# A recurrence's level in one matmul burst for each unit and step, and the merge's GELUs ordered behind the level's copies

## The chip, the cores and the metric

The kernel runs on one core of a Trainium2 chip. Time is the device time of one execution in microseconds (us). A run of the kernel before gave 1525.88 us as the median of three (1525.83 to 1526.22). The five engines have a queue each, worked off in order: TensorE (PE, matmuls), VectorE (DVE), ScalarE (ACT), GpSimd (POOL) and SyncE (SP); here POOL and SP mostly start DMAs.

## The reference

One layer of a hybrid decoder, batch 1, 1024 positions, width 1024, all in float32:

```
h    = rms_norm(x);  proj = h @ w_in            # RWKV r,k,v and low-rank parts | S5 input u | two gates
g_rwkv, g_s5 = split(sigmoid(proj[...] + b_gate))
o_rwkv = rwkv7_branch(...) @ w_branch_rwkv      # 8 heads of 64: S = S*w + (S a) b^T + v k^T ; y = S r
y      = gelu(s5_scan(u));  o_s5 = (y * sigmoid(y @ w_glu + b_glu)) @ w_branch_s5
x = x + rms_norm((g_rwkv * o_rwkv + g_s5 * o_s5) @ w_out)
x = x + rms_norm((gelu(gate) * val) @ w_down)   # gated MLP, width-3 convolution over time before the gelu
```

## The kernel before

**Three stages.** The input projection with the S5 scan comes first (to about 370 us), then the RWKV recurrence (about 370 to 770 us), then the MLP. The change lies in the recurrence.

**The recurrence.** The 8 heads are worked off in four passes, i = 0 to 3: one group of four heads for one half of the time axis each. A pass holds two units u of two heads. Time is cut into chunks of 64 positions, 8 in a pass. A pass goes through these parts:

- `rwkv_front` (prep, on PE, DVE, ACT): decay factors, the normalised keys (L736 to L741 make the operands `ar` and `bk`), and the products of all pairs of positions within a chunk (matmuls L752, masked by DVE L754 into `gr`). L760 stores the part that has to be inverted (`md`).
- `rwkv_inv`: the triangular systems of all chunks are solved for blocks of 32 by 62 small DVE operations that hang on each other (L810 and L812, 31 of each). POOL stores the result (`xd`, L815) and loads it back into `gr` (L822).
- `rwkv_nat`: transposes of `bk` and of the values (L782 to L792).
- `rwkv_level` joins the blocks of 32 to inverses of 64. DVE transposes (L835), then come two steps: matmuls of 32x32 (L838) whose results ACT copies to SBUF (L839), then matmuls L840 on these copies, whose results ACT copies into `gr` (L841).
- `rwkv_chain`: eight chunks one after the other, each in three stages: a (L888, L870), b (L899, L901) and c (L906, L911), with small copies by ACT and DVE between. After every second chunk `moments` makes means and squares (L924 to L927; the square is ACT's L926).

In the text "level 2" is `rwkv_level` of pass 2, while the prep of pass 3 runs beside it.

**The fill.** All the small matmuls wait for other engines. In their gaps PE does k-steps: three matmuls of 128x128 on 128x512 (L180 to L182) of the large products. Fill in pass 2: the last gate tiles, then `merge`. `merge` first makes gate tiles; with the second and the third of them it also emits GELUs of the S5 result for batches 0, 1 and 2, 3 (`s5_y`: DMA, then GELU L1254; `s5_split`: ACT's cast L1261 to the high part `hh`, DVE's subtraction L1262 to the low part `hl`). After the third gate tile comes the first GLU tile (`MGAP`), whose four k-steps read the four pairs `hh`, `hl`. The buffers `ev` for the GELUs are three.

**What sets the order.** PE's order is written out by the program's own planner, `drive`. Lanes (chain, two prep lanes) yield how much work they have issued, when they may go on, and a weight; a lane's work takes 0.8 x work x weight from a credit, and each k-step gives 0.68 back. While the credit is below zero only fill is emitted. The order on the other engines is set by a scheduler from priorities (fill loads and weights above chain, chain above prep) and its own model of times; a manual dependency only orders one instruction behind another on the same engine. `s5_y` orders each GELU behind `self.squared`, an instruction that `rwkv_front` sets (its Square, L700). GELU needs a table of ACT's that is loaded ahead of the first one (ACT_TABLE_LOAD).

Of the kernel before, what the change touches and what calls it, by code (L numbers as in the profile page):

```python
# [73 lines left out]
class Kern:  # L74
# [749 lines left out]
    def rwkv_level(self, d, spare):  # L824

        A, V = self.nc.scalar, self.nc.vector
        mm = self.nc.tensor.matmul
        gr = d["gr"]
        p0 = self.chk(1).rearrange("p (u c t) -> p u c t", u=2, t=32)
        p0, p1 = [p0[:, u] for u in range(2)], [self.chb().rearrange("p (c t) -> p c t", t=32) for u in range(2)]  # L830
        xz = (self.tg("x", 1, pool=self.rka) if spare else self.tg("ld", NLD)).rearrange("p (u c t) -> p u c t", u=2, t=32)
        top, bot = [[slice(64 * h + o, 64 * h + o + 32) for h in range(2)] for o in (0, 32)]
        t0, t1 = slice(0, 32), slice(32, 64)
        for h, sl in enumerate(top):
            self.levelled = V.transpose(xz[sl].rearrange("p u c t -> p (u c) t"), gr[sl, :, :, h, t0].rearrange("p u c t -> p (u c) t"))  # L835
        yield 0, T_LT
        kw = dict(stop=True, skip_group_check=True)
        steps = ((lambda u, c, h: mm(p1[u][bot[h], c], gr[top[h], u, c, h, t1], xz[top[h], u, c], start=c == 0, **kw),  # L838
                  lambda u, h: A.copy(xz[bot[h], u], p1[u][bot[h], 0:8])),  # L839
                 (lambda u, c, h: mm(p0[u][top[h], c], xz[bot[h], u, c], gr[bot[h], u, c, h, t1], start=c == 0, **kw),  # L840
                  lambda u, h: A.copy(gr[top[h], u, :, h, t1], p0[u][top[h], 0:8])))  # L841
        for step, evict in steps:
            for u in range(2):
                for c in range(8):
                    for h in range(2):
                        step(u, c, h)
                    if c % 4 == 3:
                        yield 0.3, 0.3, 2.0
                for h in range(2):
                    evict(u, h)  # L850
            yield 0, T_LV

    def rwkv_chain(self, d):
# [1339 lines left out]
```

## Time and profile before

| what | value |
|---|---|
| median of the runs | 1525.88 us (1525.83 to 1526.22) |
| profiled execution, its own time | 1524.13 us |
| its span | 1522.3 us |
| PE busy | 1469.8 us (97%) |
| DVE, ACT, POOL busy | 1158.5 (76%), 726.6 (48%), 180.2 us (12%) |

A row of a timeline gives start and duration in us, engine, line, operation, output <- input with their shapes, the number of instructions taken together (x), and in brackets how long the engine was idle before and which engine, tile and line ended it. A small matmul counts as two or more records, so a burst of 8 reads x16. In the table by stretches the columns are the stretch and its length, busy time and instructions of PE, its weight loads (PEld), DVE, ACT and POOL, the clock granted to PE (1.00 is full), the share of the DMA engines, and GB/s.

### The profile page before, as it was taken

What the parts mean: (1) busy time and instruction counts of PE and PEld (TensorE: products, weight loads), DVE (VectorE), ACT (ScalarE), POOL (GpSimd) and SP (SyncE); (2) the same over time, 40 slices, a digit from 0 to 9 for tenths busy, and PEclk for the clock granted to TensorE, in tenths of its full rate; (3) what the DMA queues carried; (4) which work ended last, traced back from release to release, by engine and by line L of the source; (5) the groups of instructions that cost most, each with busy time, mean ns of one, the idle gap of its engine ahead of it and who ended that gap; (6) DMA issues with size and microseconds to landing.
All of it is one profiled execution on the core that took longest, in us unless ns stands there. A gap on an engine that the chain in (4) does not pass through costs nothing.

```text
span 1522.3 us, 23902 instructions
## 1 busy us (share of the span) xinstructions
PE 1469.8 (97%) x8804; PEld 1166.1 (77%) x8804; DVE 1158.5 (76%) x2157; ACT 726.6 (48%) x1209; POOL 180.2 (12%) x340
## 2 busy tenths in 40 slices
PE   7999999999999998999999999999999999999997
PEld 5788787787677675666788778888888887888875
DVE  7989974765655594975767888888888888698767
ACT  5465444331453434556635555555555555444451
POOL 0022111124021232030110010000000000000000
PEclk9999999999999998999999999999999999999999
DMA  6455344444332446452456575233333336944712
GB/s 211 135 154 159 98 139 145 143 135 152 107 124 96 128 120 192 146 167 70 157 189 199 182 242 180 93 108 117 113 110 117 112 109 225 333 154 138 246 59 111
DMA packets 121558, 225.26 MB, mean 148 GB/s; under 512 B 31024, under 2 KB 37168, under 8 KB 121440
## 3 DMA queue, kind: packets, MB, share of 16 engines
q1 hardware_dynamic: 90576, 154.77, 32.5%
q0 software_dynamic: 21024, 64.71, 12.9%
q10 hardware_dynamic: 9840, 4.24, 1.1%
q8 instruction: 69, 1.13, 0.3%
q14 instruction: 49, 0.40, 0.1%
HBM read 164.16 MB, written 57.41 MB: 146 GB/s over the span
## 4 chain that ended last, share of the span: by engine, by line
PE 44%; DVE 4%; DMA 4%; ACT 1%; issue 1%; SPq 0%; DVEq 0%; ACTq 0%
PE d L1779 8%; PE rp L1600 5%; PE rp L1602 5%; PE rp L1601 5%; PE mm L1602 2%; PE mm L1600 2%; PE mm L1601 2%; DMA st<-in_w_down_dram 2%; PE ch L181 1%; PE mm L180 1%; PE ch L182 1%; PE mm L181 1%; PE gm L180 1%; PE ch L180 1%; PE mm L182 1%
## 5 line engine op out<-in xcount | busy, mean ns | idle before, releaser
L180 PE MATMUL gm<-hh,wh 128*128 128x512 f32 x672 | 283.1, 421 | 1.9 <-DVE ev L1057 1.9
L181 PE MATMUL gm<-hl,wh 128*128 128x512 f32 x672 | 264.9, 394 | 0.1
L182 PE MATMUL gm<-hh,wl 128*128 128x512 f32 x672 | 264.7, 394 | 0.0
L160 ACT CAST wh<-wf 128x512 fp32r<-128x512 f32 x181 | 111.9, 619 | 171.5 <-PE gm L181 88.5
L161 DVE TENSOR_TENSOR wl<-wf,wh 128x512 fp32r<-128x512 f32 x181 | 124.3, 690 | 86.5 <-ACT wh L160 84.5
L180 PEld LDWEIGHTS gm<-hh,wh 128*128 128x128 f32 x672 | 127.0, 189 | 34.3 <-issue 4.0
L182 PEld LDWEIGHTS gm<-hh,wl 128*128 128x128 f32 x672 | 127.0, 189 | 28.1
L181 PEld LDWEIGHTS gm<-hl,wh 128*128 128x128 f32 x672 | 127.4, 190 | 22.5 <-DVE hl L246 1.0
L1779 PE MATMUL d<-xh,wl 128*128 128x512 f32 x308 | 113.5, 392 | 2.1 <-DVE wl L246 2.1
L1779 PE MATMUL d<-xh,wh 128*128 128x512 f32 x308 | 113.9, 393 | 1.1 <-DVE zg L1630 1.1
L1779 PE MATMUL d<-xl,wh 128*128 128x512 f32 x308 | 113.4, 392 | 0.6 <-DVE xl L246 0.6
L1600 PE MATMUL rp<-t,h 128*128 128x512 f32 x252 | 98.3, 390 | 1.4 <-ACT p L1614 1.4
L1602 PE MATMUL rp<-t,l 128*128 128x512 f32 x252 | 98.0, 389 | 0.0
L1601 PE MATMUL rp<-t,h 128*128 128x512 f32 x252 | 98.0, 389 | 0.0
L1779 PEld LDWEIGHTS d<-xh,wl 128*128 128x128 f32 x308 | 58.1, 189 | 15.1 <-DVE wl L246 2.9
L1779 PEld LDWEIGHTS d<-xh,wh 128*128 128x128 f32 x308 | 57.8, 189 | 14.2 <-DVE zg L1630 1.5
L246 DVE TENSOR_TENSOR l<-r,h 128x1024 fp32r<-128x1024 f32 (+1 forms) x40 | 38.9, 971 | 38.9 <-ACT h L245 38.9
L1779 PEld LDWEIGHTS d<-xl,wh 128*128 128x128 f32 x308 | 58.2, 189 | 13.2 <-DVE xl L246 0.9
L245 ACT CAST h<-r 128x1024 fp32r<-128x1024 f32 (+1 forms) x40 | 33.9, 849 | 69.5 <-PE rp L1601 67.2
L1621 DVE SCALAR_TENSOR_TENSOR y<-zv,vecs,y 128x1023 f32<-128x1023 f32 (+1 forms) x42 | 53.7, 1280 | 10.2 <-ACT y L1619 10.2
L1600 PEld LDWEIGHTS rp<-t,h 128*128 128x128 f32 x252 | 47.3, 188 | 11.9 <-ACT p L1614 2.2
L1601 PEld LDWEIGHTS rp<-t,h 128*128 128x128 f32 x252 | 47.3, 188 | 9.8
(476 smaller groups left out, 3338.1 us busy)
## 6 DMA issues: line engine op xcount, KB each, us to landing
r<-in_w_up_dram SPq DMA_DIRECT2D x42, 512.0 KB, 3.5
wf<-in_w_in_dram SPq DMA_DIRECT2D x72, 256.0 KB, 3.1
st<-in_w_down_dram SPq DMA_DIRECT2D x55, 256.0 KB, 4.3
st<-ACT SPq DMA_DIRECT2D x44, 256.0 KB, 4.2
ACT<-y POOLq DMA_DIRECT2D x21, 512.0 KB, 2.9
GT<-ev POOLq DMA_DIRECT2D x32, 256.0 KB, 3.5
wf<-in_w_br_dram SPq DMA_DIRECT2D x32, 256.0 KB, 3.4
wf<-in_w_out_dram SPq DMA_DIRECT2D x32, 256.0 KB, 2.8
```

What stands on the lines that cost most here:

```text
L160: self.last_wh = nc.scalar.copy(h[:, :n], f[:, :n])
L161: low = nc.vector.tensor_tensor(l[:, :n], f[:, :n], h[:, :n].bitcast(F32), ALU.subtract)
L180: mm(ps, a, xh[k], start=a0, stop=False)
L181: mm(ps, a, xl[k], start=False, stop=False)
L182: mm(ps, b, xh[k], start=False, stop=z0)
L245: a = self.nc.scalar.copy(hi, x)
L246: self.split_ops = a, (eng or self.nc.vector).tensor_tensor(lo, x, hi.bitcast(F32), ALU.subtract)
L1600: mm(ps, wh[:, c], xh, start=first and k == 0, stop=False, skip_group_check=True)
L1601: mm(ps, wh[:, c], xl, start=False, stop=False, skip_group_check=True)
L1602: mm(ps, wl[:, c], xh, start=False, stop=k == 3, skip_group_check=True)
L1621: V.scalar_tensor_tensor(y[:, lag:], z[:, 0:1024 - lag], self.vec(nme, i), y[:, lag:], ALU.mult, ALU.add)
L1779: mm(ps, w[:, c], y[:, x], start=start and k == 0, stop=stop and k == 2, skip_group_check=True)
```

## The change

Two places in `rwkv_level`:

```
                 for c in range(8):
                     for h in range(2):
                         step(u, c, h)
-                    if c % 4 == 3:
-                        yield 0.3, 0.3, 2.0
+                yield 0.6, 0.3, 1.5
                 for h in range(2):
-                    evict(u, h)
+                    self.squared = evict(u, h)
             yield 0, T_LV
```

The 16 matmuls of a unit and step are issued together, and one yield stands for two. A unit and step then takes 0.8 x 0.6 x 1.5 = 0.72 from the credit where it took 2 x 0.8 x 0.3 x 2.0 = 0.96. `self.squared` now is also set by the level's copies, and so GELUs that are emitted later stand behind the last copy emitted. The file is one line shorter: L850 and later lines have a number lower by one after the change (GELU L1253, cast L1260, split L1261, square L925).

What moves in level 2 is seen at three places. First ACT, from the end of the gate tiles on; `chb` is what L838 wrote, `ev` the GELUs' buffers, `hh` the high parts. Before:

```order
L1139 ACTIVATE ev_6167<-gm_6096,hb_b_gate 128x512
L1254 ACT_TABLE_LOAD
L1254 ACTIVATE ev_6274<-ev_6274 128x512
L1254 ACTIVATE ev_6281<-ev_6281 128x512
L1261 CAST hh_6277<-ev_6274 128x512
L160 CAST wh_6566<-wf_6568 128x512
L1261 CAST hh_6284<-ev_6281 128x512
L1254 ACTIVATE ev_6336<-ev_6336 128x512
L839 COPY x_6155<-chb_6154 32x256
L1261 CAST hh_6339<-ev_6336 128x512
```

The level's copies stood behind the table load and three GELUs. After the change the same GELUs come in chunk 1 of the chain, behind its square:

```order
L925 ACTIVATE ar_4784<-yn_6426 128x256
L1253 ACT_TABLE_LOAD
L1253 ACTIVATE ev_6469<-ev_6469 128x512
L160 CAST wh_6804<-wf_6806 128x512
L1260 CAST hh_6472<-ev_6469 128x512
L1253 ACTIVATE ev_6476<-ev_6476 128x512
L1253 ACTIVATE ev_6533<-ev_6533 128x512
L1260 CAST hh_6479<-ev_6476 128x512
L1260 CAST hh_6536<-ev_6533 128x512
L902 COPY UV_5672<-chb_6611 64x128
L873 COPY p_1213_6621<-chk_6610 128x128
L1253 ACTIVATE ev_6540<-ev_6540 128x512
```

Second PE, where the first GLU tile (`gm_6652`) reads them, in chunk 2 after the change; `chk_6610` and `chb_6611` are that chunk's stages b and c:

```order
L900 MATMUL chk_6610<-S_2614,ar_4784 64x64 x4
L180 MATMUL gm_6652<-hh_6472,wh_6646 128x512
L181 MATMUL gm_6652<-hl_6473,wh_6646 128x512
L182 MATMUL gm_6652<-hh_6472,wl_6647 128x512
L180 MATMUL gm_6652<-hh_6479,wh_6646 128x512
L181 MATMUL gm_6652<-hl_6480,wh_6646 128x512
L182 MATMUL gm_6652<-hh_6479,wl_6647 128x512
L905 MATMUL chk_6610<-UV_5672,gr_4604 64x64 x4
L910 MATMUL chb_6611<-UV_5672,bkn_5671 64x64 x4
L180 MATMUL gm_6652<-hh_6536,wh_6646 128x512
```

Between stage c of chunk 1 (L905) and this tile PE has four k-steps and the stages a and b of chunk 2. Before, the first GLU tile stood in chunk 0, and its GELUs ahead of the chain.

Third DVE, at the end of level 2's inverse (tiles `x_5413` before, `x_5426` after). Before:

```order
L737 SCALAR_TENSOR_TENSOR gr_5718<-ld_5722,vecs,rp_6006 128x512
L810 TENSOR_TENSOR tm_5509<-x_5413,mt_5412 128x16
L246 TENSOR_TENSOR hl_6061<-ld_5696,hh_6060 128x512
L812 TENSOR_TENSOR x_5413<-x_5413,tm_5509 128x16
L246 TENSOR_TENSOR hl_6051<-hl_6051,hh_6050 128x512
L246 TENSOR_TENSOR hl_6065<-ld_5699,hh_6064 128x512
L737 SCALAR_TENSOR_TENSOR gr_5718<-ld_5731,vecs,rp_6019 128x512
```

L738, L739 and four of L741 followed. After the change these stand between the inverse's operations, from L737 on; a piece of it:

```order
L810 TENSOR_TENSOR tm_5504<-x_5426,mt_5425 128x98
L741 SCALAR_TENSOR_TENSOR bk_5829<-gr_5687,ld_5693 64x8x64
L812 TENSOR_TENSOR x_5426<-x_5426,tm_5504 128x2x7x7
L741 SCALAR_TENSOR_TENSOR bk_5829<-gr_5687,ld_5702 64x8x64
L810 TENSOR_TENSOR tm_5507<-x_5426,mt_5425 128x84
L741 SCALAR_TENSOR_TENSOR bk_5829<-gr_5687,ld_5702 64x8x64
L812 TENSOR_TENSOR x_5426<-x_5426,tm_5507 128x2x7x6
L246 TENSOR_TENSOR hl_6081<-ld_5665,hh_6080 128x512
L810 TENSOR_TENSOR tm_5510<-x_5426,mt_5425 128x70
L246 TENSOR_TENSOR hl_6085<-ld_5668,hh_6084 128x512
```

Of the 14 operations L737 to L741 and L246, all now stand ahead of the inverse's last row; before, two did. On POOL the three stores of `md` that follow them now stand ahead of the loads L822, where they stood behind, and the GELUs' loads come later.

## The prediction

> **What bounds the kernel now.** First the page: the span and the busy shares.
>
> ```profile
> span 1522.3 us, 23902 instructions
> PE 1469.8 (97%) x8804; PEld 1166.1 (77%) x8804; DVE 1158.5 (76%) x2157; ACT 726.6 (48%) x1209; POOL 180.2 (12%) x340
> ```
>
> TensorE (PE) is the bound: 52.5 us of 1522.3 are idle, and the matmuls themselves stay the same in number and size. So the change can move the time in three ways: the cost of switching between small and large matmuls, PE's waits, and the clock that PE is granted. Next the table by stretches around level 2, the third of the four passes through the edited loop (from about 576 us), and one stretch in level 1; the ninth column is the granted clock.
>
> ```profile
> 460.00:464.00 4.00, 4.00 (x12) 2.88 (x10) 3.90 (x18) 0.69 (x1) 0.55 (x1) 0.58 0.19 70
> 588.00:592.00 4.00, 2.31 (x18) 1.13 (x18) 3.80 (x6) 3.43 (x7) 2.83 (x5) 0.71 0.43 122
> 592.00:596.00 4.00, 4.00 (x38) 2.52 (x38) 1.65 (x2) 1.44 (x3) 2.38 (x6) 0.50 0.60 166
> 596.00:600.00 4.00, 4.00 (x25) 2.78 (x24) 0.00 (x0) 1.44 (x4) 0.94 (x2) 0.51 1.00 230
> ```
>
> From 588 to 600 PE runs at about half speed: 4 x (0.29 + 0.50 + 0.49) = 5.1 us are lost. In 460 to 464 it is 4 x 0.42 = 1.7 us. What came before the slow stretch stands in PE's timeline:
>
> ```profile
> 589.28 0.24 PE L840 MATMUL chk<-gr,x 32*32 32x32 f32 x2 [3.42 <-ACT x L839]
> 589.94 0.63 PE L840 MATMUL chk<-gr,x 32*32 32x32 f32 x14 [0.41 <-ACT x L839]
> ```
>
> PE waits 3.42 + 0.41 = 3.8 us for the copies of L839, the largest wait of the recurrence. ScalarE's (ACT's) timeline says what is ahead of them, and VectorE's (DVE's) when the last result of that block is ready:
>
> ```profile
> 581.66 1.28 ACT L1254 ACT_TABLE_LOAD   x1 [6.03 <-issue]
> 582.96 1.38 ACT L1254 ACTIVATE ev<-ev 128x512 f32<-128x512 f32 x2
> 584.24 1.09 ACT L1261 CAST hh<-ev 128x512 fp32r<-128x512 f32 x1
> 585.23 0.62 ACT L160 CAST wh<-wf 128x512 fp32r<-128x512 f32 x1
> 588.86 1.02 ACT L839 COPY x<-chb 32x256 f32<-32x256 f32 x3
> 591.65 1.06 ACT L1261 CAST hh<-ev 128x512 fp32r<-128x512 f32 x1
> 593.22 1.04 DVE L1262 TENSOR_TENSOR hl<-ev,hh 128x512 fp32r<-128x512 f32 x1
> ```
>
> The merge's table load, GELUs and casts run where the level needs its copies. From table load to last split the block takes 594.26 - 581.66 = 12.6 us.
>
> **The change part by part. The bursts.** Level 0 shows the price of cutting a burst in two:
>
> ```profile
> 376.35 0.44 PE L838 MATMUL chb<-ld,gr 32*32 32x32 f32 x16
> 376.72 0.50 PE L180 MATMUL gm<-hh,wh 128*128 128x512 f32 x1
> 377.06 0.40 PE L181 MATMUL gm<-hl,wh 128*128 128x512 f32 x1
> 377.29 0.39 PE L182 MATMUL gm<-hh,wl 128*128 128x512 f32 x1
> 377.61 0.44 PE L838 MATMUL chb<-ld,gr 32*32 32x32 f32 x16
> ```
>
> Large matmuls start 0.23 us apart (377.06 to 377.29). The one behind a burst holds 0.34 (0.11 more), the one ahead of the next 0.32 (0.09 more): 0.20 us for each visit, while the small matmuls cost the same either way. 32 bursts become 16; in the order, 15 stretches of small matmuls fewer are left. **-3.0 us** (-1.6 if only the 0.11 behind a burst goes, -3.4 if all 16 and a little more).
>
> **The GELUs leave the level.** With them go the waits of 3.8 us and the slow clock: **-3.8** and **-5.1**. The copies now stand behind one tanh that is done well before, and PE has over 4 us of other work between the last L838 and the first L840 (a set of L752, four k-steps and L763), so I leave nothing of this wait. Level 3's wait should go too, since its inverse (DVE) gets all of the new stalls below as extra time: **-1.0** (0 to -1.0).
>
> ```profile
> L838 PE MATMUL chb<-ld,gr 32*32 32x32 f32 x64 | 2.0, 194 | 1.0 <-DVE ld L835 1.0
> ```
>
> **The inverse of level 2 gets company.** This is the side of the change that its words don't tell: in the new order the preparation of pass 3 (L737 to L741) and four splits (L246) stand inside level 2's inverse on DVE, where nearly all of it followed before.
>
> ```profile
> 556.38 1.04 PE L736 MATMUL rp<-csts,gr 128*128 128x128 f32 x8
> 557.86 0.74 DVE L737 SCALAR_TENSOR_TENSOR gr<-ld,vecs,rp 128x512 f32<-128x512 f32 x1
> 559.21 0.19 DVE L812 TENSOR_TENSOR x<-x,tm 128x16 f32<-128x16 f32 x1
> 560.22 0.68 DVE L246 TENSOR_TENSOR hl<-ld,hh 128x512 fp32r<-128x512 f32 x1
> 562.09 1.28 DVE L738 SCALAR_TENSOR_TENSOR ar<-gr 128x512 f32<-128x512 f32 x2
> 563.29 1.28 DVE L739 SCALAR_TENSOR_TENSOR gr<-ld,gr 128x512 f32<-128x512 f32 x2
> 565.70 1.98 DVE L741 SCALAR_TENSOR_TENSOR bk<-gr,ld 64x512 f32<-64x512 f32 x3
> 571.66 0.69 DVE L835 STREAM_TRANSPOSE x<-gr 32x512 f32<-32x512 f32 x1
> 559.69 1.29 POOL L815 DMA_DIRECT2D xd<-x  x2 [0.25 <-DVE x L812]
> 565.79 4.64 POOL L822 DMA_DIRECT2D gr<-xd  x8 [1.09 <-DMA xd<-x]
> 566.88 1.44 PE L752 MATMUL rp<-ar,bk 64*64 64x128 f32 x32
> 576.10 0.44 PE L838 MATMUL chb<-x,gr 32*32 32x32 f32 x16
> ```
>
> The inverse used to end at 559.4. The first L737 can't run before L736 (PE has no earlier place for it), so about 557.6, and now 19 operations of the inverse stand behind it: some 4.6 us (an estimate of 0.24 each, where the last and smallest takes 0.19), and the 14 others (two of which stood there before), both L737 among them, come to 2 x 0.74 + 1.28 + 1.28 + 4 x 0.66 + 4 x 0.68 = 9.4 by these rows, about 8.8 as neighbouring rows overlap a little. It ends near 571.0, 11.6 us later. From its end to the loads of L822 took 6.4 us and those 4.6 more; both transposes of L835 add 1.4, so L838 can start at about 583.4. Three DMAs of `md` now stand ahead of L822 on POOL's queue, and they end in the 2 us in which it waits for `xd` anyway. PE comes to L838 at 576.1 + 1.7 (a set of L752 and a k-step, 1.0 and 0.7, now stand ahead of it; useful work) + a wait of 1.5 at the first L752, for the last L741 of its unit. So PE waits **+1.5** (0 to 2.5) and 583.4 - 579.3 = about 4; I take **+3.7** (1.5 to 5), as a load may land sooner.
>
> **The GELUs have a new neighbour.** They now stand behind chunk 1's square, and the first GLU tile, whose 4 k-steps eat their splits, stands two chain stages behind that on PE.
>
> ```profile
> 605.60 0.45 PE L906 MATMUL chk<-UV,gr 128*64 128x64 f32 x8
> 610.18 0.50 PE L180 MATMUL gm<-hh,wh 128*128 128x512 f32 x1
> 611.78 0.45 PE L906 MATMUL chk<-UV,gr 128*64 128x64 f32 x7
> 612.27 0.53 ACT L909 COPY yn<-chk 64x128 f32<-64x128 f32 x2 [1.42 <-PE chk L906]
> 615.56 0.42 ACT L926 ACTIVATE ar<-yn 128x256 f32<-128x256 f32 x1 [0.25 <-DVE yn L925]
> ```
>
> PE reaches that tile 610.18 - 605.60 = 4.6 us after stage c of chunk 1. The square ends 4.2 us after it in this trace; three operations of 0.42 behind copies that end after 1.0 would be 2.3. I take 3.0 for the table load, so PE arrives 1.6 us into the block. By the rows above the block then gives its splits at 1.3 + 0.7 + 0.6 + 1.1 + 1.0 = 4.7 (first), 7.1, 8.1 and, with chunk 2's two small copies ahead of the fourth GELU, 10.3. PE ends the tile at 10.8; of the 9.2 us since it arrived, 4 x 0.7 + 0.4 for stage c are work. **+6.0** (5.0 to 7.2). In the old order the tile came 10 us after the last split, which is the cover that is gone.
>
> **The clock after the new waits.** The trace has two prices: 1.7 us (level 1) and 5.1 (level 2, after 3.8 us of waiting among small matmuls). L838's wait is of the latter length and place: I take two steps of 1.7, **+3.4** (0 to 5.1). The GLU tile's wait is cut into pieces by k-steps: **+1.7** (0 to 3.4).
>
> Sum: -3.0 - 3.8 - 5.1 - 1.0 = -12.9, and 1.5 + 3.7 + 6.0 + 3.4 + 1.7 = +16.3: **+3.4 us**. The profiled execution took 1524.13, so 1527.5 in its frame; the median of the runs is 1.75 above it: **1529.3 us**.
>
> **The rivals. Waits are swapped, the clock holds.** A wait does not have to lower the clock:
>
> ```profile
> 532.00:536.00 4.00, 2.68 (x18) 2.15 (x17) 3.94 (x11) 3.95 (x9) 0.54 (x1) 1.00 0.10 29
> 536.00:540.00 4.00, 4.00 (x23) 3.40 (x23) 3.97 (x10) 1.10 (x3) 0.00 (x0) 1.00 0.61 191
> ```
>
> Here 1.3 us of idle PE left it at 1.00. If both new waits do the same, 5.1 goes: -1.7, **1524.2**. Against it: 3.4 us of waiting did lower it, and L838's wait is as long. [...]
>
> **The inverse is in time: faster.** If the moved operations fill pauses on DVE or L737 comes earlier, and the inverse ends by about 566, L838 does not wait, and +1.5, +3.7 and +3.4 go: -12.9 + 6.0 + 1.7 = -5.2, **1520.7**. For it: DVE is 76% busy. Against it: the tail's rows follow each other without a pause, so what is put between them makes them later.
>
> **Both waits at their upper ends: slower.** If L738 or the `md` DMAs are later than I put them and the slow clock returns as in level 2, 2.5 + 5 + 7.2 + 5.1 + 3.4 = 23.2, less 12.9: +10.3, **1536.2**. That the change does not do what it says is no case: the order shows the bursts whole and the GELUs behind the copies.
>
> **How the numbers follow.** Forecast 0.42, swapped 0.22, faster 0.21, both at their ends 0.15. A measurement of this kernel tells about 0.2% (3.05 us) from no change. Faster: 0.19 of the third case and 0.06 of the second, 0.25. Slower: 0.29 of the forecast, the fourth, and 0.01 of the second, 0.45. Within: the rest, 0.30. The range goes from 1519 (inverse in time, GLU tile a little earlier) to 1536; the forecast's own is 1525.5 to 1533.
>
> **What would show it.** Right: L840 without a wait in level 2, the clock at 1.00 behind it; the last L812 of level 2's inverse some 11 us later against L736; L838 of level 2 waiting 2 to 5 us for L835; the first GLU tile waiting 5 to 7 us for DVE L1261 or ACT L1260 (one line lower than now). Wrong: no wait at L838, or a GLU tile that waits under 3 us, or bursts of 16 that cost more than two of 8.

## The result, and the profile after

| | before | after | ratio, 95% interval |
|---|---|---|---|
| first comparison (6 runs each) | 1525.86 us (1520.19 to 1528.31) | 1544.34 us (1533.94 to 1549.93) | 1.0127 (1.0098 to 1.0155) |
| second (13 and 4 runs) | 1521.66 us (1518.18 to 1527.84) | 1538.66 us (1535.59 to 1544.30) | 1.0117 (1.0079 to 1.0155) |

The change is slower by 17 to 18.5 us. The forecast was slower by 3.4 (1529.3, range 1519 to 1536): the sign is right, the size is far off.

The first profile after is of an execution of 1549.93 us, the second of the same program of 1536.04. Their heads:

```profile
span 1548.1 us, 23889 instructions
PE 1480.1 (96%) x8804; PEld 1179.2 (76%) x8804; DVE 1159.8 (75%) x2157; ACT 726.9 (47%) x1209; POOL 182.1 (12%) x340
```

```profile
span 1534.3 us, 23889 instructions
PE 1468.5 (96%) x8804; PEld 1171.8 (76%) x8804; DVE 1160.4 (76%) x2157; ACT 727.5 (47%) x1209; POOL 182.2 (12%) x340
```

Idle PE is span less busy: 52.5 us before, 68.0 and 65.8 after. So 13.3 to 15.5 us more of each execution is PE waiting. Busy PE is 1469.8 before, 1480.1 and 1468.5 after: the same program with the same matmuls differs by 11.6 us, and the granted clock averaged 0.977 in one and 0.984 in the other (0.991 before). In a stretch of half clock of the first the large matmuls start 0.43 us apart (585.53 to 585.96), at full clock 0.23 (577.77 to 578.00). Where these stretches fall differs between the two executions; the waits of the recurrence, 29.5 and 30.3 us, hardly do.

The table of PE's waits in the recurrence, after the change:

```profile
PE gm L180 <- ACT hh L250: 6.1, 1, 6.1
PE chk L900 <- ACT p L873: 6.0, 2, 5.7
PE chb L838 <- DVE x L835: 5.3, 2, 4.8
PE chb L898 <- DVE p L890: 4.0, 2, 2.8
PE chk L887 <- ACT p L873: 2.8, 4, 1.3
PE chk L887 <- DVE S L912: 2.7, 3, 1.3
PE chk L840 <- ACT gr L841: 0.3, 1, 0.3
```

All its rows between 370 and 780 us add up to 29.5 us (30.3 in the second profile); before it was 13.6, with these rows among them:

```profile
PE chk L840 <- ACT x L839: 3.8, 2, 3.4
PE chk L888 <- ACT p L874: 2.4, 4, 0.9
PE chb L838 <- DVE ld L835: 1.0, 1, 1.0
```

The prediction took out L840's 3.8 and L838's 1.0, and both are gone. But there are three large waits where two were forecast, and several of 1 to 3 us in the chain.

**The three waits.** First L838 of level 2, in DVE's, POOL's and PE's timelines: the end of the inverse, the reload, the transposes, the matmuls.

```profile
568.54 0.19 DVE L812 TENSOR_TENSOR x<-x,tm 128x16 f32<-128x16 f32 x1
576.23 4.60 POOL L822 DMA_DIRECT2D gr<-xd  x8 [1.37 <-DMA xd<-x]
582.46 1.43 DVE L835 STREAM_TRANSPOSE x<-gr 32x512 f32<-32x512 f32 x2 [3.63 <-DMA gr<-xd]
583.21 0.25 PE L838 MATMUL chb<-x,gr 32*32 32x32 f32 x2 [4.82 <-DVE x L835]
583.95 1.06 PE L838 MATMUL chb<-x,gr 32*32 32x32 f32 x30 [0.49 <-DVE x L835]
```

Second the GELU block in chunk 1 and 2. PE stops at stage b of chunk 2, one step ahead of the GLU tile:

```profile
612.74 1.28 ACT L1253 ACT_TABLE_LOAD   x1
617.11 2.02 ACT L1260 CAST hh<-ev 128x512 fp32r<-128x512 f32 x2
619.42 0.27 ACT L873 COPY p<-chk 128x128 f32<-128x128 f32 x1
619.74 0.69 PE L900 MATMUL chk<-S,ar 64*64 64x64 f32 x8 [5.65 <-ACT p L873]
```

L873 copies the next chunk's values out of the same PSUM tile that L900 writes, and it stands behind the table load, three GELUs and three casts. Third, 42 us after this one ends, the last GLU tile. Its own GELU (`s5_y` once more, L1253) reads a load that POOL issues behind the eight reloads of the next inverse and four other loads:

```profile
650.50 4.63 POOL L822 DMA_DIRECT2D gr<-xd  x8 [2.63 <-issue]
657.84 0.54 POOL L1252 DMA_DIRECT2D ev<-YU  x1 [0.54 <-DVE hl L251]
665.27 0.63 ACT L1253 ACTIVATE ev<-ev 128x512 f32<-128x512 f32 x1 [3.57 <-DMA ev<-YU]
667.00 0.63 ACT L250 ACTIVATE hh<-ev 128x512 fp32r<-128x512 f32 x1 [1.10 <-DVE ev L1273]
667.68 0.80 PE L180 MATMUL gm<-hh,wh 128*128 128x512 f32 x1 [6.14 <-ACT hh L250]
```

POOL was through with those loads at 657.30; for the last 0.54 us it waited until the split L251 of the GLU tile before had read the buffer `ev`. The GELU could start at 665.27, 7.4 us after the issue.

**The clock behind them.** In the table by stretches (ninth column) each of the three is followed by half clock:

```profile
584.00:588.00 4.00, 4.00 (x75) 3.12 (x79) 0.00 (x0) 1.09 (x3) 0.00 (x0) 0.50 0.19 60
588.00:592.00 4.00, 4.00 (x38) 3.23 (x35) 1.43 (x3) 0.99 (x2) 1.40 (x3) 0.73 0.32 96
620.00:624.00 4.00, 4.00 (x28) 2.84 (x28) 3.73 (x12) 1.78 (x3) 0.54 (x1) 0.50 0.27 70
668.00:672.00 4.00, 4.00 (x14) 3.10 (x14) 2.24 (x4) 1.82 (x4) 0.00 (x0) 0.50 0.50 174
```

That is 2.0 + 1.1, 2.0 and 2.0 us lost. Each stretch of half clock in the profiles of before and of the first execution after, 18 in all, lasted 3.4, 6.8 or 10.2 us (to 0.05 us); counted in steps of 3.4 us (windows, in the expectations), that is one, two or three. In both profiles after, two steps lie at each of the three places (583.35 to 590.15, 617.45 to 624.30 and 665.25 to 672.05 in the first; in part they pass while PE still waits). Before, one place of level 2 had three (589.65 to 599.90).

**What the edit does to a level.** Counted in PE's order, from the first L838 of a level to the first matmul of its chain (k-steps in levels 0, 1, 2, 3):

```
before                              12 12 12 12
the change                           8  7  9  8
one burst, weight 2.0                8  8  8  8
one burst, weight 3.0                8  9 12  8
two bursts, weight 2.0, new order   12 12 12 12
```

A yield of 0.48 of credit is paid back by one k-step (0.68), so two yields bought two k-steps for each unit and step, and one yield of 0.72 mostly buys one. A level loses about four k-steps, 2.7 us (4 x 0.68; the three matmuls of a k-step start 0.23 us apart), and with them go 2.7 us of cover for everything that other engines do meanwhile. One more thing shows in the order: without `self.squared = evict(...)` the change gives the same program on all five engines. The second half of the change moves nothing.

### The profile page after: what moved, and what is told of

It reads as the page before. It is cut to its first block, busy times and chain, and to the rows that moved or that the text cites. A ratio compares the mean times of both kernels' runs of the same rounds, so it can differ in the third digit from the quotient of the medians.

```text
span 1548.1 us, 23889 instructions
## 1 busy us (share of the span) xinstructions
PE 1480.1 (96%) x8804; PEld 1179.2 (76%) x8804; DVE 1159.8 (75%) x2157; ACT 726.9 (47%) x1209; POOL 182.1 (12%) x340
## 3 DMA queue, kind: packets, MB, share of 16 engines
q1 hardware_dynamic: 90576, 154.77, 31.5%
## 4 chain that ended last, share of the span: by engine, by line
PE 74%; DVE 10%; DMA 8%; issue 4%; ACT 3%; POOL 1%; SPq 0%; DVEq 0%; POOLq 0%; ACTq 0%
PE d L1778 10%; PE gm L180 9%; PE gm L181 8%; PE gm L182 8%; PE rp L1599 5%; PE rp L1600 5%; PE rp L1601 5%; PE mm L1600 2%; PE mm L1601 2%; PE mm L1599 2%; DVE wl L161 2%; DMA wf<-in_w_up_dram 1%; DMA st<-in_w_down_dram 1%; PE ch L181 1%; PE ch L182 1%
## 5 line engine op out<-in xcount | busy, mean ns | idle before, releaser
L180 PE MATMUL gm<-hh,wh 128*128 128x512 f32 x672 | 285.0, 424 | 8.0 <-ACT hh L250 6.1
L180 PEld LDWEIGHTS gm<-hh,wh 128*128 128x128 f32 x672 | 128.5, 191 | 41.4 <-ACT hh L250 6.6
L1778 PEld LDWEIGHTS d<-xh,wl 128*128 128x128 f32 x308 | 57.8, 188 | 13.6 <-DVE wl L246 1.6
L246 DVE TENSOR_TENSOR l<-r,h 128x1024 fp32r<-128x1024 f32 (+1 forms) x40 | 38.9, 971 | 38.7 <-ACT h L245 38.6
L1620 DVE SCALAR_TENSOR_TENSOR y<-zv,vecs,y 128x1023 f32<-128x1023 f32 (+1 forms) x42 | 53.8, 1281 | 10.2 <-ACT y L1618 10.2
L1599 PEld LDWEIGHTS rp<-t,h 128*128 128x128 f32 x252 | 47.2, 188 | 12.2 <-ACT p L1613 2.4
L1601 PEld LDWEIGHTS rp<-t,l 128*128 128x128 f32 x252 | 47.3, 188 | 9.8
```

The costliest lines, as they stand in the source:

```text
L180: mm(ps, a, xh[k], start=a0, stop=False)
L246: self.split_ops = a, (eng or self.nc.vector).tensor_tensor(lo, x, hi.bitcast(F32), ALU.subtract)
L1599: mm(ps, wh[:, c], xh, start=first and k == 0, stop=False, skip_group_check=True)
L1601: mm(ps, wl[:, c], xh, start=False, stop=k == 3, skip_group_check=True)
L1620: V.scalar_tensor_tensor(y[:, lag:], z[:, 0:1024 - lag], self.vec(nme, i), y[:, lag:], ALU.mult, ALU.add)
L1778: mm(ps, w[:, c], y[:, x], start=start and k == 0, stop=stop and k == 2, skip_group_check=True)
```

## The experiments

In kernels of the experiments that have more lines, the lines behind the insertion have numbers up to 6 higher. The ratios come from the single runs and are not quotients of the medians.

### The change once more

No edit.

> The change as it is, timed and profiled a second time. Theory A (the merged bursts halve the k-steps that stand in a level, so the merge and its GELUs slide into the chain and meet waits there): the same waits in the same places as in the first profile, at L838 some 5 us, at L900 of chunk 2 some 5.7, at the fourth GLU tile's user (L180 behind L250) some 6, while the half-clock windows may lie elsewhere; time 1534 to 1550. Theory B (the clock does it: long runs of 32x32 matmuls lower the granted clock): windows of half clock stand behind every level's bursts again, in each of the four levels. If most of the windows lie outside the levels and move between the two profiles, B is wrong and the spread between executions comes from where the windows fall.

Measured: 1538.66 us, ratio 1.0117 (1.0079 to 1.0155). The waits of its profile:

```profile
PE gm L180 <- ACT hh L250: 6.6, 1, 6.6
PE chk L900 <- ACT p L873: 6.0, 2, 5.7
PE chb L838 <- DVE x L835: 5.1, 2, 4.5
```

Within 0.5 us of the first profile. The stretches of half clock: two steps behind each of the three waits in both profiles; six other places are common to both, five of them outside the recurrence, and elsewhere the first profile has eight steps more, the second one. Theory B, that the long bursts lower the clock, has little support: no stretch follows the bursts of levels 0 or 3 in either profile, and at level 1's there are three steps in the first profile and none in the second.

### The new order alone

```
-                    evict(u, h)
+                    self.squared = evict(u, h)
```

> Two bursts and two yields as before; only the GELUs' order behind the level's last copy emitted is added, so PE's order is that of before word for word. On ACT two of the copies L839 come ahead of the table load, the others still between the GELUs. Theory A: the wait of 3.8 us at L840 shrinks to 1 to 3 us, and the slow clock behind it is shorter or gone: 1517 to 1524. Theory B says nothing else here, as the bursts are those of before.

Measured: 1529.48 us against 1521.66, 1.0049 (1.0033 to 1.0066): slower. The wait moved from one copy to the other, and a new one came:

```profile
PE chk L840 <- ACT gr L841: 4.5, 3, 3.1
PE rp L968 <- DVE yn L960: 3.8, 2, 3.1
```

With two bursts the new order does act: two copies L839 pass ahead of the table load, but the block then stands ahead of L841. Of L840's 4.5 us, 3.1 fall in level 2. All waits of the recurrence add up to 18.8 us instead of 13.6. The expectation was wrong.

### One burst with the old credit

```
-                    if c % 4 == 3:
-                        yield 0.3, 0.3, 2.0
+                yield 0.6, 0.3, 2.0
```

> One burst for each unit and step, with the weight 2.0 instead of 1.5, so that a level takes the same credit as before (0.96 for each unit and step), and without the new order (with it the program is the same). The table load now stands behind the first p copy of the chain, in chunk 0 instead of chunk 1. Theory A: the GELUs still meet the chain, with a wait of 4 to 6 us at an L873 copy that stands behind them; L838 still waits, since the inverse has the same company; 1528 to 1545. Theory B: as slow as the change, 1540 to 1550, with the windows behind the bursts.

Measured: 1533.70, 1.0083 (1.0052 to 1.0115), waits 26.4 us: L180 behind L250 5.1, L838 4.7, stage c of chunk 2 behind ACT's copy of UV 2.8. The weight is not the cause; 0.96 of credit in one yield buys 8 k-steps too.

### One burst with the old number of k-steps

```
+                yield 0.6, 0.3, 3.0
...
+                    self.squared = evict(u, h)
```

> One burst for each unit and step with weight 3.0 (1.44 of credit, two k-steps, as the two bursts of before had), and the new order, so a level has as many k-steps as before and the merge starts about as early as before. Theory A: the level's first copies L839 stand ahead of the table load, the GLU tiles come after their GELUs, and the switches saved are worth 3 us: 1512 to 1524, if the inverse (which still has its company) is in time. Theory B: the bursts of 16 lower the clock whatever stands around them: 1535 or more.

Measured: 1533.07, 1.0071 (1.0042 to 1.0099), outside theory A's range. Only level 2 got its 12 k-steps back; the L900 wait is gone, but L838 waits 6.9 us and L887 5.6 us for the state S. Levels 0 and 1 were still short.

### The inverse kept alone

```
+            self.inverted = V.tensor_tensor(x[:, :, 0:ns, q + 1:32], ...)
...
+        op = V.scalar_tensor_tensor(kk, k, self.vec("k_k", p), kb, ALU.mult, ALU.mult)
+        if i == 3:
+            self.tc.add_manual_dep(op.ins, self.inverted.ins.name, ORDER)
```

and the same dependency for the low parts in `merge_values`.

> The change, with the preparation of pass 3 (L737 and what hangs on it) and the four splits of the merge's values ordered behind the last operation of level 2's inverse on DVE; nothing else is asked for. Theory A (the company in the inverse is what L838 waits for): the wait of 5 us at L838 is gone or under 1.5, the two half-clock windows behind it too, and the waits at L900 (5.7) and L180 behind L250 (6.6) stay: 1529 to 1535, against 1538.7 of the change. Rival: the wait only moves, to L752 and its masks, which now come later than their old place: L838 or L752 wait 4 to 6 us in sum and the time stays at 1536 to 1541.

Measured: 1542.52, 1.0140 (1.0101 to 1.0180). L838 no longer waits, but the rival is right, the wait has moved:

```profile
576.42 0.69 DVE L766 TENSOR_TENSOR ld<-rp,ld 128x512 f32<-128x512 f32 x1 [4.55 <-DMA ld<-RKV]
577.16 1.98 PE L754 MATMUL rp<-ar,bk 64*64 64x128 f32 x30 [6.32 <-DVE ld L766]
```

(L766 is L764 and L754 is L752 of the kernel before.) The transposes for L838 end at 569.4, 5 us before PE would come to it without this wait. In this program the load of v for pass 3 came to stand behind the reloads on POOL.

### The inverse alone, and v by another queue

```
-        v = ld(self.RKV[8 + p], G)
+        v = ld(self.RKV[8 + p])
```

on top of the one before.

> The change with level 2's inverse kept alone, as in an earlier run where the wait moved to L752 because the load of v for pass 3 then stood behind the inverse's reloads on POOL; here this load goes by SP's queue. Theory A (the company in the inverse sets L838's wait): no wait over 1.5 us at L838 and at L752 of level 2; idle time down by 5, 1530 to 1535. Rival (each link that is freed shows the next, since the level comes too early for all of them): again 4 us or more in sum somewhere between L752 and L840 of level 2, 1536 to 1542.

Measured: 1536.74 against 1524.44, 1.0085 (1.0053 to 1.0117). Now the inverse ends 20.3 us ahead of L838 (here L840), not 14.5, and L838 waits for nothing (L814 and L837 are L812 and L835):

```profile
553.75 0.19 DVE L814 TENSOR_TENSOR x<-x,tm 128x16 f32<-128x16 f32 x1
568.88 1.42 DVE L837 STREAM_TRANSPOSE x<-gr 32x512 f32<-32x512 f32 x2
574.27 0.69 PE L840 MATMUL chb<-x,gr 32*32 32x32 f32 x32
```

The transposes are ready 4 us ahead of L838. So the cause of L838's wait is the company in the inverse, as the prediction had it. At L752 2.1 + 1.0 us are left. Against the change's 1.0117 the gain is 0.3%, about 5 us, with intervals that overlap, and the time is above theory A's 1530 to 1535; the waits fell from 30.3 to 26.8.

### The inverse alone, and the GLU tiles' loads by another queue

```
-lambda: self.s5_y(self.ev(s8), m, 0)
+lambda: self.s5_y(self.ev(s8), m, 0, self.nc.sync)
```

on top of the inverse kept alone.

> As the one with the inverse alone, and the second loads of the S5 result (the ones that the GLU tiles' own GELUs read) go by SP's queue instead of POOL's, where the last of them stood behind the eight reloads of the inverse and four other loads. Theory A: the wait of 6.6 us at L180 behind L250 goes as well: 1521 to 1529. Rival: the load is late for its buffer and not for its queue, so L180 still waits over 4 us and the time is within 2 us of the kernel with the inverse alone.

Measured: 1538.83, 1.0119 (1.0081 to 1.0157), against 1542.52 for the inverse alone in the same comparison (the intervals overlap); theory A's 1521 to 1529 did not come. The load is issued at 651.3, in the run with the inverse alone at 652.1. Seen from PE it is 4.2 us earlier, since the last stage c ahead of it (L907) starts at 655.0 here and at 651.7 there. The third wait shrinks:

```profile
PE gm L180 <- ACT hh L250: 1.2, 1, 1.2
PE gm L181 <- DVE hl L251: 0.6, 1, 0.6
PE rp L969 <- DVE yn L961: 2.6, 1, 2.6
```

From 6.3 to 1.8, so the late issue was the cause. Whether POOL's queue or the buffer made it late is not told apart: all these loads changed queue, and the buffer came free at 648.4 instead of 651.8. A wait of 2.6 at the transposes of this pass's results (`yn`) takes part of its place, and all waits stay at 31.5.

### The kernel before with the GELUs' loads by another queue

The same edit in the kernel before, for the first loads too.

> The kernel before with all loads of the S5 result in the merge on SP's queue. In the kernel before ACT stood idle for 6 us ahead of the table load, and the first load was issued on POOL only 6.2 us before it, behind the inverse's reloads. Theory A: the GELUs start some 3 us earlier, so that the copies L839 are late by 0 to 2 us instead of 3.8, and with less waiting the three windows of half clock behind it are one or none: 1513 to 1520 (before: 1521.7). Rival: the table load waits for something else than the load, and the time stays at 1520 to 1524.

Measured: 1528.62 against 1520.39, 1.0046 (1.0022 to 1.0070): slower, the rival's side and beyond. L840 waits 5.2 us for L839, and L968 4.9.

### All repairs together

> One burst for each unit and step with weight 3.0 (as many k-steps in a level as before), the inverse kept alone, and the loads on SP's queue. Theory A: the waits of 6.9 us at L838 and 2.5 at L180 go, those in the chain behind S (L887, 5.6 us) may stay: 1516 to 1526, against 1533 with the weight 3.0 alone. Rival (the chain's waits set the time, not L838): 1528 to 1535.

Measured: 1542.23, 1.0122 (1.0066 to 1.0179), above theory A and the rival. One wait of 8.1 us for the load of v, as with the inverse alone, and 6.1 us in the chain for S. Each repair gave another order, and all but the one that also moved v brought a new wait with it.

### One level at a time

The merged burst with weight 1.5 only in the levels named (`self.nat` is the pass):

```
+                    if self.nat not in (3,) and c % 4 == 3:
                         yield 0.3, 0.3, 2.0
+                if self.nat in (3,):
+                    yield 0.6, 0.3, 1.5
```

> Only level 0 merges its bursts (weight 1.5); the other three levels keep two bursts. Theory A2 (after the runs so far: each merged level is four k-steps shorter, so everything behind it meets the loads and the other engines at another time, and the harm is done where the order of DVE, ACT and POOL then falls badly): already this one edit, 200 us ahead of level 2, puts the preparation of pass 3 into level 2's inverse, so L838 of level 2 waits 4 to 7 us, while the copies L839 stand ahead of the table load and L840 waits under 2: 1522 to 1530. Rival (the harm is done by the merged bursts of level 2 itself): 1517 to 1521, and no wait at L838 of level 2.

> Only level 2 merges its bursts. Theory A2: the inverse of level 2 stays as it was, so no wait at L838 of level 2, and the GELUs stay in the level with a wait of 2 to 5 us at L840; 1516 to 1526, about as before. Rival (the harm is done by the merged bursts of level 2 itself): 1530 or more, with waits at L900 or L180 behind L250.

> Only level 3 merges its bursts; everything up to 650 us is the kernel before, word for word. Theory A2: the four merges save 4 x 0.3 = 1.2 us, the last pass's chain meets the early GELUs four k-steps sooner, 1518 to 1524. Rival: level 3 carries part of the harm (waits in its chain of 3 us more than before): 1525 or more.

> Levels 0, 1 and 3 merge their bursts, level 2 keeps two. Theory A2: as level 0 alone with the harm of level 1 added; the table load stands behind the level's first copy of step 2, the inverse has company, L838 of level 2 waits 4 to 7 us, the chain 3 to 6: 1525 to 1535. Rival (the merged bursts of level 2 itself): 1515 to 1520, as 12 merges are saved.

All against 1522.40 (29 runs; by the medians the last row would be 1.0072):

| merged in | us | ratio, 95% interval | PE's waits, 370 to 780 us |
|---|---|---|---|
| level 0 | 1530.38 | 1.0051 (1.0031 to 1.0071) | 20.6 |
| level 2 | 1530.65 | 1.0052 (1.0030 to 1.0074) | 22.0 |
| level 3 | 1519.24 | 0.9975 (0.9953 to 0.9996) | 12.9 |
| levels 0, 1, 3 | 1533.32 | 1.0053 (1.0031 to 1.0076) | 23.9 |

Level 0's four merges alone change the order inside level 2's inverse, 200 us later, but they bring little company: 5 of the 14 operations L737 to L741 and L246 stand in it, where the kernel before has 2 and the change 14. L838 of level 2 does not wait; the wait is at L840 behind L841 (3.2 us there, 5.4 over all levels), so the expectation was wrong. With levels 0, 1 and 3 merged all 14 stand in it, and L838 waits 4.7. Level 2 alone leaves the inverse as it was (2 of 14, no wait at L838) and turns L840's wait there of 3.8 into one of 4.8 behind L841, with 2.0 more in level 3 and 4.9 at L968; its time is above the expected 1516 to 1526. So over these versions L838 waits where the company is there, and not where it is not. Only level 3, behind which no other level comes, gains: the one version that beats the kernel before, by 0.25%, just clear of no change.

### Unread matmuls in the idle gaps

```
+            if evict is steps[1][1] and self.nat == 2:
+                for _ in range(14):
+                    mm(pk[:, 0:512], self.h[0][0][0][:, 0:128], self.h[0][0][0], start=True, stop=True, skip_group_check=True)
```

`pk` is the PSUM tile that L840 fills afterwards. The first kernel has these 14 in the version with level 3 merged, the second in the kernel before; the third has 20 ahead of L838 in the change.

> Level 3 alone merges its bursts (the kernel that came out at 0.9975 of before), and PE does 14 large matmuls of 0.23 us, 3.2 us in all, whose results nobody reads, ahead of the first L840 of level 2, where it otherwise stands idle for 3.8 us. They wait for nothing that is late, so they cost nothing while the wait lasts. Theory A (an idle PE is what the clock answers with half speed): the wait left at L840 is under 1 us, the three windows of half clock behind it are gone, 5 us with them: 1511 to 1517, against 1519.2. Rival (the windows come from the small matmuls, or from where they happen to fall): three windows at the same place, and 1518 to 1523.

> The kernel before with the same 14 unread matmuls ahead of the first L840 of level 2, and nothing else. Theory A: the three windows behind the wait are gone: 1515 to 1519, against 1522. Rival: 1521 to 1525.

> The change with 20 unread matmuls of 0.23 us (4.6 us) ahead of the first L838 of level 2, where PE waits 5 us. Theory A: the wait left there is under 1 us and the two windows behind it are gone, worth 3 us: 1533 to 1537, against 1538.7; the waits at L900 and L180 keep theirs. Rival: windows stay there, 1537 to 1542.

Measured, against 1524.44: 1525.78, 1.0014 (1.0000 to 1.0028); 1526.37, 1.0023 (1.0001 to 1.0046); 1533.54, 1.0071 (1.0047 to 1.0095). In the kernel before with the 14, and in the change with the 20, the clock at the place of the wait:

```profile
592.00:596.00 4.00, 3.10 (x50) 1.81 (x51) 2.38 (x4) 2.43 (x4) 1.63 (x4) 1.00 0.58 158
```

```profile
576.00:580.00 4.00, 4.00 (x88) 3.12 (x81) 1.07 (x2) 1.46 (x4) 0.09 (x1) 1.00 0.63 204
580.00:584.00 4.00, 4.00 (x45) 2.57 (x43) 1.60 (x3) 1.27 (x3) 2.55 (x5) 1.00 0.78 222
```

It stays at 1.00 in both (from 588 to 600 in the first, from 572 to 588 in the second), where it was 0.50 for 10.2 us and for 6.8. The small matmuls are the same, and PE does 3.10 to 4.00 us of work in each 4.00 of these rows: at these two places the half clock went with PE's waiting. In the change this is worth 0.46% (1.0117 to 1.0071, the intervals overlap a little), though the third wait grew to 8.8 us, and the time is in theory A's range of 1533 to 1537. In the other two it gained nothing: with the added matmuls ACT's and DVE's later work stands in another order, with new waits of 2.3 and 2.5 us. In the kernel before with the 14, half clock shows at other places (large matmuls of 0.63 us, 0.43 apart, between 685.6 and 690.7), and the mean clock over all runs is 0.990 and 0.989 in these two, against 0.989 before. The 1511 to 1519 expected there did not come.

## Why the prediction was right or wrong

- **Bursts, -3.0 (-1.6 to -3.4).** Right in kind, too small. A burst of 16 holds PE for 380.56 - 379.94 = 0.62 us, less than two of 0.37, and one switch of 0.20 is saved besides: 2 x 0.57 - 0.82 = 0.32 for each pair, about 5 us for 16.

```profile
379.94 0.69 PE L838 MATMUL chb<-ld,gr 32*32 32x32 f32 x32
380.56 0.50 PE L180 MATMUL gm<-hh,wh 128*128 128x512 f32 x1
```

- **L840's wait and its slow clock, -3.8 and -5.1; level 3's wait, -1.0.** Right: 0.3 us is left at L840, and L838 of level 3 does not wait. But the slow clock came back behind the other waits.
- **L838 of level 2, +1.5 and +3.7.** Right in the mechanism: 1.1 us at L752 and 5.3 at L838 (5.1 in the second profile), just above the upper end of 5 that was given for the latter. The inverse ended 13.7 us after L736's start where 14.6 was worked out; the run with the inverse and v apart and the levels tried one by one show the mechanism.
- **The GELU block, +6.0 at the first GLU tile.** Right in size (5.7), wrong in place. The step looked at what the tile needs and not at what else stands in ACT's queue behind the block: the copy L873 of chunk 3's values, for which stage b of chunk 2 waits. The first GLU tile itself waits for nothing, which the prediction had named as a sign of being wrong; that the size agrees is in part luck.
- **The step that failed: counting the waits.** The prediction followed the first use of the S5 result and stopped there. The GLU tiles load and GELU it a second time; the text ahead of the prediction says that the GELUs' loads come later on POOL, and the sum has no term for it. That is the 6.1 to 6.6 us of the third wait. And levels 0 and 1 were costed as a pure gain, with no cover named: in level 1's chain the scan of the next prep now stands ahead of the chain's sum on DVE and waits for its load while PE waits 2.8 us (before, PE waited 0.6 us there, for the state S).

```profile
518.84 1.22 DVE L718 TENSOR_TENSOR_SCAN ld<-csts,ld 128x512 f32<-128x512 f32 x1 [4.32 <-DMA ld<-TZ]
519.98 0.26 DVE L890 TENSOR_TENSOR p<-p,chk 128x128 f32<-128x128 f32 x1
520.30 0.27 PE L898 MATMUL chb<-p,gr 64*64 64x64 f32 x2 [2.82 <-DVE p L890]
```

  In sum the forecast had PE's idle time up by 11.2 - 4.8 = 6.4 us; it went up by 13.3 to 15.5. About 8 us of that is the third wait and level 1's chain.
- **"That the change does not do what it says is no case."** Wrong for its second half. The GELUs stand behind the level because levels with 8 k-steps end before the merge starts; the new dependency changes nothing in the order.
- **The clock, +3.4 and +1.7.** Right for the two waits that were priced (3.1 and 2.0 us measured). Not priced were the third wait's 2.0, one step of 3.4 us (1.7 us lost) that follows level 1's 2.8 us of waiting in both profiles, and what falls elsewhere: over all runs the mean clock went from 0.990 to 0.982. With the 5.1 taken out the forecast had the clock at a net 0. Of the measured 17.0 to 18.5 us, 13.3 to 15.5 are waits and -5 the bursts; the rest, some 8 us by this estimate, is the clock. So this term of the sum failed as well: 3.7 us of it follow the two waits that were not counted, and the rest falls at places that no wait here explains.
- **The rivals.** "Waits are swapped, the clock holds" is refuted by the three stretches, "the inverse is in time" by L838's wait. "Both waits at their upper ends" gave 1536.2 for another reason than what happened; a third wait was on no list.

The time follows the waits over the twelve kernels with over 5 us of new waits and no unread matmuls. With 0.32 us given back for each merged pair, a microsecond of PE's waiting costs 1.1 to 1.7: the change (17.0 + 5) / (30.3 - 13.6) = 1.3, level 0 alone (8.0 + 1.3) / 7.0 = 1.3, the order alone 7.8 / 5.2 = 1.5. The part above one is, as far as the profiles show, the half clock that follows; no run here separates the two for all waits.

What stays open: why the first comparison's executions spread over 16 us (in the two executions of this program that were profiled the waits agree and only the steps of half clock fall differently); why the clock also falls where PE is busy all the time, as in level 1 at 460 to 464 before (0.58, with PE at 4.00 of 4.00); and which of the small waits in the chain (1.0 to 1.3 us each) comes from which moved operation.

## What to carry to other kernels

Where a planner fills gaps with work that it pays for by yields, merging two yields also removes work from the gap: count what lies in each gap before and after, and treat each shorter gap as a loss of cover for every engine. In a program whose order is one long chain of decisions, follow a moved transfer or operation through every use of its data, the second one too, and through whatever stands behind it in its queue. And test an edit place by place: of the three levels that were merged alone, two lose and one gains.

## What the runs showed of the hardware that was not expected

- The 18 stretches of half clock in the profiles of before and of the first execution after lasted 3.4, 6.8 or 10.2 us. In the change one step of 3.4 followed a PE wait of 2.8 us (521.90 to 525.30) and two went with each wait of 4.5 to 6.6; before, three followed a wait of 3.8 us that ended in small matmuls. With unread matmuls in the gap the clock was 1.00 there, in the kernel before from 588 to 600 and in the change from 572 to 588.
- The same program with waits equal within 0.5 us had 1468.5 and 1480.1 us of busy PE in two executions.
- A load `ev<-YU` of 256 KB, which takes 4.6 us to land in the median of its eight, came 7.4 us after its issue (657.84 to 665.27) while the share of the DMA engines stood at 1.03 and 1.05:

```profile
656.00:660.00 4.00, 4.00 (x34) 2.92 (x34) 3.46 (x10) 2.62 (x7) 2.94 (x7) 1.00 1.03 304
660.00:664.00 4.00, 1.54 (x10) 0.89 (x10) 3.16 (x12) 1.64 (x4) 1.55 (x3) 1.00 1.05 391
```
